# Laying out the solved blocks of a delta-rule recurrence: TensorE products with the unit matrix in place of transfers through DRAM

## The chip, the cores and the metric

One Trainium2 chip, one core of it, float32 throughout. The metric is the device time of one launch in microseconds (us). The kernel before has a median of 3638.72 us over three runs (3634.84 to 3644.53). The kernel computes two whole blocks of a network; the change touches one stage of the first block that takes some 400 us of the time.

## The reference, cut to what matters

The first block mixes tokens by a recurrence (RWKV-7), run forward and backward over 256 context and then 512 latent tokens, 8 heads of 64 in each direction:

```python
def wkv_bidir(r, k_d, v, kk, w, a, state0):
    xs = (tm(both(r)), tm(per(w)), tm(per(k_d)), tm(both(v)), tm(both(-kk)), tm(per(kk[:, :, None] * a)))

    def step(s, inp):
        r_t, w_t, k_t, v_t, aa_t, bb_t = inp
        sa = jnp.einsum('dbhij,dbhj->dbhi', s, aa_t)
        s = s * w_t[..., None, :] + sa[..., :, None] * bb_t[..., None, :] + v_t[..., :, None] * k_t[..., None, :]
        y_t = jnp.einsum('dbhij,dbhj->dbhi', s, r_t)
        return s, y_t

    state, ys = lax.scan(step, state0, xs)
...
    y_c, state_c = wkv_bidir(r_c, k_c, v_c, kk_c, w_c, a_c, state0)
    y_l, _ = wkv_bidir(r_l, k_l, v_l, kk_l, w_l, a_l, state_c)
```

What follows it (group norm, a Fourier mix, a mixture of experts, a second block with sparse attention) is not touched.

## The kernel before, in words

The recurrence is computed in chunks of 64 tokens. A *unit* is 128 tokens (two chunks) in both directions; units 0 and 1 are the context, 2 to 5 the latent tokens. Inside a chunk the tokens depend on each other through a lower triangular matrix per head, which has to be inverted. The kernel does it for all 32 pairs of head and chunk of a unit at once, in parts with names:

- **a1** (`load`, `lora`, `expo1`, `expo2`, `keys1`): the loads of k, kn and r, the decay and rate products, their running sum and its two exponentials.
- **a2** (`keys2` to `keys4`, `gram`, `move`, `turn`): scaled keys on DVE (L651 to L667); the Gram products on PE (L683) and their 24 (context: 16) masks on DVE (L684 to L688); `move` brings the diagonal blocks of 32x32 into the tile `N` through DRAM (`scN`, L695, L698); `turn` transposes the keys (L706).
- **s** (`solve`): 31 steps of two DVE instructions each (L722, L724) that invert the 64 diagonal blocks of the unit, 32 rows of them in `Fm`.
- **b** (`back`): brings the inverted blocks from `Fm` into the layouts that the next products read. Two DVE copies (L733) and nine transfers through DRAM: `scF` (L737), `scE` (L738), `fe` (L739, L740) and the diagonal of `fd` (L745).
- **m** (`merge`, `merge2`): per unit 32 products of 32x32 from `lm` and `fe` (L754), copied to `re` (L755), then 32 more (L764), copied into `fd` (L765): the off-diagonal blocks.
- the **chain** (`fill`, `X`, `V`, `St`, `Y`, L790 to L867): the state's own way through the unit, which needs `v` (loaded at L787), `fd`, `ar`, `bkt`; `St` (L848) makes the next state, `Y` (L866, L867) the output of latent units.

`head()` plays unit 0's a1, a2 and s beside the last projection products. `wkv()` then plays b and m of unit 0 and a2 of unit 1, and after that one *step* for each unit u, in which stand chain(u), s, b and m of unit u+1, a2 of u+2 and a1 of u+3. Each piece has a position between u and u+1 from the table `PL`, and `play` writes the pieces in the order of positions: s of u+1 from 0.127 to 0.312, b at 0.838, the Gram parts of u+2 from 0.885 to 0.942, `turn` at 0.932, m at 0.999. A scheduler then settles the order of instructions inside each engine's queue, and each engine runs its queue in that order. Transfers are issued by SP, in its queue's order.

`ttile` hands out work tiles of 4 KB per partition by turns: 8 in one pool, 4 in another (`nt`, L592). A new tile waits until its predecessor in the same place has been read.

Of the kernel before, what the change touches and what calls it, by code (L numbers as in the profile page):

```python
# [8 lines left out]
F = mybir.dt.float32  # L9
R = mybir.dt.float32r  # L10
I32 = mybir.dt.int32
AF = mybir.ActivationFunctionType
# [86 lines left out]
class Blk1:  # L99
# [432 lines left out]
    def open_wkv(self):  # L532

        tc, nc, I = self.tc, self.nc, self.i
        self.yD = [self.dram.tile([512, 512], F, name=f"yD{d}") for d in range(2)]
        self.prD = self.dram.tile([128, 4, 4, 2, 128], F, name="prD")
        self.vtD = [self.dram.tile([512, 512], F, name=f"vtD{d}") for d in range(2)]
        self.gnD = [[self.dram.tile([128, 512], F, name=f"gnD{d}{u}") for u in range(2, 5)] for d in range(2)]
        wc = self.wA = self.ctx.enter_context(tc.tile_pool(name="wA", bufs=1, side="right", reuse_waits="tile"))
        self.wB = None  # L540
        self.fd = [wc.tile([128, 4, 4, 64], F, name="fd0")]
        nc.gpsimd.memset(self.fd[0], 0.0)
        self.sv = {}
        self.ntt = 0
        self.U = [self.unit(u) for u in range(6)]
# [43 lines left out]

        return (self.wB if u % 3 else self.wA).tile(shape, F, name=name, tag=f"{name}{u % 3}", bufs=1)  # L590

    nt = (8, 4)  # L592

    def unit(self, u):

        nc = self.nc
# [35 lines left out]

        def expo2():
            c = S["c"]
            e1, e2 = S["e1"], S["e2"] = self.tt("e1"), self.tt("e2")
            nc.scalar.activation(e1, c, AF.Exp, scale=-KAP)
            nc.scalar.activation(e2, c, AF.Exp, scale=KAP)
            pcc = S["pc"] = self.wA.tile([128, 4, 4], F, name="pcc", tag="pcc", bufs=4)
            nc.gpsimd.tensor_copy(pcc, e1[:, :, :, 63])
# [69 lines left out]
        def solve(a, b):  # L709

            def f():
                N = S["N"]
                if a == 0:
                    room = self.ttile([128, 2, 16, 32], "Fm")
                    S["F"], S["T"] = room[:, 0], room[:, 1]
                    nc.gpsimd.memset(S["F"], 0.0)
                    for j in range(2):
                        nc.gpsimd.memset(S["F"][j * 64:(j + 1) * 64].rearrange("p s t -> p (s t)")[:, j::34], 1.0)
                Fm, tm = S["F"], S["T"]
                for s in range(a, min(b, 31)):  # L720
                    w, m = 31 - s, s // 2 + 1
# [2 lines left out]
                    nc.vector.tensor_tensor(Fm[:, :m, s + 1:], Fm[:, :m, s + 1:], tm[:, :m, :w], op=OP.add)  # L724
            return f

        def back():
            Fm = S["F"]

            re = S["re"] = self.ttile([128, 32, 32], "re")  # L730
            fe = S["fe"] = self.ttile([128, 32, 32], "fe")
            for a in range(2):
                nc.vector.tensor_copy(re[32:64].rearrange("p t (i a) -> p a i t", a=2)[:, a], Fm[a * 64:a * 64 + 32])  # L733
            scf = self.dram.tile([2, 32, 32, 32], F, name="scF", tag="scF", bufs=3)
            sce = self.dram.tile([32, 32, 32], F, name="scE", tag="scE", bufs=3)
            for a in range(2):
                nc.sync.dma_start(scf.rearrange("b c (i a) t -> a (b c) i t", a=2)[a], Fm[a * 64:(a + 1) * 64])  # L737
            nc.sync.dma_start(sce, re[32:64])  # L738
            nc.sync.dma_start(fe[0:32], scf[1].rearrange("c s t -> s c t"))  # L739
            nc.sync.dma_start(fe[64:96], sce.rearrange("c a b -> a c b"))  # L740
            fd = S["fd"] = self.fd[u % 3]
            for b in range(2):
                for h in range(2):
                    q = h * 64 + 32 * b
                    nc.sync.dma_start(fd[q:q + 32, :, :, 32 * b:32 * b + 32].rearrange("p a n t -> p (a n) t"),  # L745
                                      scf[b, h * 16:h * 16 + 16].rearrange("c s t -> s c t"))

        def merge(q):
            def f():
                re, fe, lm = S["re"], S["fe"], S["lm"].rearrange("p h a n t -> p (h a n) t")  # L750
                p = self.psum()
                for j in range(16):
                    c = q * 16 + j
                    nc.tensor.matmul(p[0:32, j * 32:(j + 1) * 32], lm[64:96, c, 32:64], fe[64:96, c, :], start=True, stop=True)  # L754
                nc.scalar.activation(re[0:32, q * 16:(q + 1) * 16], p[0:32].rearrange("p (c t) -> p c t", t=32), AF.Copy)  # L755
            return f

        def merge2(q):
            def f():
                re, fe = S["re"], S["fe"]  # L760
                p = self.psum()
                for j in range(16):
                    c = q * 16 + j
                    nc.tensor.matmul(p[0:32, j * 32:(j + 1) * 32], re[0:32, c, :], fe[0:32, c, :], start=True, stop=True)  # L764
                nc.scalar.activation(S["fd"][q * 64:q * 64 + 32, :, :, 32:64], p[0:32].rearrange("p (a n t) -> p a n t", n=4, t=32), AF.Copy)  # L765
            return f

        a2 = [keys2, keys3] + ([keys4] if lat else []) + [gram(q) for q in range(4)] + [move, turn]
        sv = list(range(32))
        return {"S": S, "a1": [load, lora(0), lora(1), expo1, expo2, keys1], "a2": a2,  # L770
                "s": [solve(a, b) for a, b in zip(sv, sv[1:])], "b": [back], "m": [merge(0), merge(1), merge2(0), merge2(1)]}

    def slab(self, d, k):
        if (d, k) not in self.sv:
# [2361 lines left out]
```

## Time and profile before

| | |
|---|---|
| median of 3 runs | 3638.72 us (3634.84 to 3644.53) |
| profiled execution, its own time | 3639.38 us |
| its span, first to last instruction | 3637.5 us |
| mean granted TensorE clock | 0.931 |
| PE busy over the span | 3310.7 us (91%) |
| DVE, ACT, POOL busy | 66%, 46%, 28% |
| the stage of the change | about 250 to 664 us |

The profile is one execution. The share of PE over the span is an average over many stages. The recurrence is one of the few in which the PE is idle for longer: of its five steps 0 to 4 (305 to 605 us) PE is busy 228 of 300 us. A step is measured here from the first L790 of a unit to the first L790 of the next, where the chain takes over the next unit. "PEclk" is the clock that TensorE was granted, as a share of 2.4 GHz; 0.50 is 1.2 GHz.

### The profile page before, as it was taken

How to read it: one execution, taken by the hardware profiler on the slowest of the kernel's cores; microseconds unless marked ns; L12 is line 12 of the kernel's file. 1: busy time of each engine (PE TensorE's matmuls, PEld its weight loads, DVE VectorE, ACT ScalarE, POOL GpSimd, SP SyncE). 2: the span in 40 equal slices, each digit the busy share in tenths (PEclk: the TensorE clock that was granted, in tenths of full speed). 3: DMA queues.
4: the chain of work that ended last, by engine and by line, in shares of the span. 5: the costliest groups of instructions: out<-in, count | busy, mean ns of one | idle time of the engine just before them, and what ended most of it. 6: DMA issues, size and time to landing. Idle time of an engine off the chain costs nothing. (4 is left out here: it accounts for less than half of the span.)

```text
span 3637.5 us, 49607 instructions
## 1 busy us (share of the span) xinstructions
PE 3310.7 (91%) x16700; PEld 2483.3 (68%) x16700; DVE 2416.8 (66%) x4743; ACT 1662.0 (46%) x2901; POOL 1017.3 (28%) x960
## 2 busy tenths in 40 slices
PE   7877589949999998999999997999999999999999
PEld 4756477646656565666666564788878878887887
DVE  6787775576978677867867776654656455456653
ACT  4634233314656555554655553444444334444442
POOL 4342122432312211201301313332421433324223
PEclk9986676969999999999999998999999999999999
DMA  7853234626889889789889987322321243222112
GB/s 259 268 162 83 63 73 124 227 81 203 297 304 314 288 307 323 259 293 320 299 286 311 308 271 249 113 81 64 88 61 53 92 141 88 76 76 82 41 53 104
DMA packets 420268, 653.41 MB, mean 180 GB/s; under 512 B 83763, under 2 KB 145264, under 8 KB 419494
## 3 DMA queue, kind: packets, MB, share of 16 engines
q1 hardware_dynamic: 414362, 633.24, 53.8%
q0 software_dynamic: 3920, 13.63, 1.2%
q10 hardware_dynamic: 1724, 3.28, 0.3%
q8 instruction: 135, 2.21, 0.3%
q14 instruction: 127, 1.04, 0.1%
HBM read 610.46 MB, written 39.61 MB: 179 GB/s over the span
## 5 line engine op out<-in xcount | busy, mean ns | idle before, releaser
L1336 DVE TENSOR_TENSOR wlo<-wraw,whi 128x1024 fp32r<-128x1024 f32 (+1 forms) x712 | 855.5, 1212 | 389.4 <-ACT whi L1332 378.0
L1332 ACT ACTIVATE whi<-wraw 128x1024 fp32r<-128x1024 f32 x712 | 741.1, 1056 | 542.7 <-PE ps L1725 141.4
L2302 PE MATMUL psg<-whi,xh 128*128 128x512 f32 (+1 forms) x1152 | 471.4, 409 | 0.8 <-ACT xh L2319 0.8
L2304 PE MATMUL psg<-whi,xl 128*128 128x512 f32 (+1 forms) x1152 | 450.5, 391 | 0.0
L2303 PE MATMUL psg<-wlo,xh 128*128 128x512 f32 (+1 forms) x1152 | 449.1, 390 | 0.3 <-DVE wlo L1336 0.3
L1747 POOL TENSOR_TENSOR ln<-ln,sg 64x256 f32<-64x256 f32 (+1 forms) x148 | 194.8, 1318 | 786.0 <-DVE ln L1746 542.8
L1338 POOL TENSOR_TENSOR wlo<-wraw,whi 128x288 fp32r<-128x288 f32 x184 | 241.3, 1313 | 578.9 <-ACT whi L1332 562.6
L1726 PE MATMUL ps<-wlo,x 128*128 128x512 f32 x864 | 349.7, 405 | 8.2 <-DVE wlo L1336 8.2
L1725 PE MATMUL ps<-whi,x 128*128 128x512 f32 x864 | 352.3, 408 | 0.0
L1721 PE MATMUL ps<-wraw,x 128*128 128x512 f32 x640 | 303.0, 616 | 0.0
L2304 PEld LDWEIGHTS psg<-whi,xl 128*128 128x128 f32 x1152 | 217.1, 188 | 42.1
L2303 PEld LDWEIGHTS psg<-wlo,xh 128*128 128x128 f32 x1152 | 217.7, 189 | 35.2 <-DVE wlo L1336 0.8
L2302 PEld LDWEIGHTS psg<-whi,xh 128*128 128x128 f32 x1152 | 217.6, 189 | 35.4 <-ACT xh L2319 1.8
L1721 PEld LDWEIGHTS ps<-wraw,x 128*128 128x128 f32 x640 | 121.9, 196 | 123.3 <-issue 117.8
L1726 PEld LDWEIGHTS ps<-wlo,x 128*128 128x128 f32 x864 | 166.2, 192 | 52.7 <-DVE wlo L1336 15.7
L1725 PEld LDWEIGHTS ps<-whi,x 128*128 128x128 f32 x864 | 166.7, 193 | 45.0 <-issue 4.8
L1725 PE MATMUL ps<-whi,a 128*128 128x512 f32 x432 | 182.1, 422 | 0.0
L1726 PE MATMUL ps<-wlo,a 128*128 128x512 f32 x432 | 178.1, 412 | 1.5 <-DVE wlo L1336 1.5
L2442 ACT ACTIVATE pexp<-pss,mx 128x128 f32<-128x128 f32 x192 | 100.9, 526 | 155.0 <-DVE mx L2437 66.6
L1721 PE MATMUL ps<-wraw,a 128*128 128x512 f32 x320 | 148.2, 604 | 0.0
L1745 ACT ACTIVATE sg<-gl 64x256 f32<-64x256 f32 (+1 forms) x148 | 61.0, 412 | 147.3 <-DVE gl L1743 140.1
L1693 POOL DMA_INDIRECT xg<-hD,idxi x37 | 46.4, 1255 | 265.6 <-PE ps L1706 239.7
(732 smaller groups left out, 6760.5 us busy)
## 6 DMA issues: line engine op xcount, KB each, us to landing
wraw<-in_w SPq DMA_DIRECT2D x768, 512.0 KB
wraw<-in_w_in SPq DMA_DIRECT2D x140, 512.0 KB
mraw<-in_w_ada SPq DMA_DIRECT2D x32, 512.0 KB
wraw<-in_w_out SPq DMA_DIRECT2D x24, 512.0 KB
wada<-in_w_ada SPq DMA_DIRECT2D x16, 512.0 KB
wraw<-in_w_mem_kv SPq DMA_DIRECT2D x16, 512.0 KB
wraw<-in_w_branch_m SPq DMA_DIRECT2D x8, 512.0 KB
wraw<-in_w_branch_b SPq DMA_DIRECT2D x8, 512.0 KB
```

Source lines behind the costliest of these rows:

```text
L1332: nc.scalar.activation(hi, raw, AF.Copy)
L1336: nc.vector.tensor_tensor(lw[:, :m], rw[:, :m], hw[:, :m].bitcast(F), op=OP.subtract)
L1338: nc.gpsimd.tensor_tensor(lw[:, m:], rw[:, m:], hw[:, m:].bitcast(F), op=OP.subtract)
L1721: nc.tensor.matmul(ps, a, w[:, k], start=s, stop=e)
L1725: nc.tensor.matmul(ps, a, hi[:, k], start=s, stop=False)
L1726: nc.tensor.matmul(ps, a, lo[:, k], start=False, stop=e and not two)
L1745: nc.scalar.activation(sg[:m], gl[:m], AF.Sigmoid, scale=1.702)
L1747: nc.gpsimd.tensor_tensor(ln[:m], ln[:m], sg[:m], op=OP.mult)
L2302: nc.tensor.matmul(p, xh[:, kk], hi[:, k, :n], start=kk == 0, stop=False)
L2303: nc.tensor.matmul(p, xh[:, kk], lo[:, k, :n], start=False, stop=False)
L2304: nc.tensor.matmul(p, xl[:, kk], hi[:, k, :n], start=False, stop=kk == kch - 1)
L2442: nc.scalar.activation(p[:, :n], s[:, :n], AF.Exp, bias=nm, scale=-1.0, accum_out=H["d"][:, i:i + 1])
```

## The change

The transfers of `back` and its two DVE copies go. In their place PE multiplies the solved blocks with the unit matrix, in two groups of products, and ACT copies the products out of PSUM:

- `back0`: 16 products and two copies give `f0`, what `merge` reads (`fe[64:96]` before).
- `back`: 32 pairs of products that accumulate, each pair 64 columns wide, and 20 copies give the diagonal of `fd` and `f1`, what `merge2` reads (`fe[0:32]` before).

All solves work in one tile `fp` with a fixed place, and its work copy `ft` is fixed, too. `fe` and `Fm` are no longer handed out by turns, `re` lies in the first 32 partitions of the unit's own `N`, and the two exponentials are written over their inputs `sw` and `cum`. A latent unit's step takes 10 tiles by turns from 10 (6 and 4) where it took 14 from 12. The position of b in `PL` stays.

```diff
@@ -540,6 +540,10 @@
         self.wB = None
         self.fd = [wc.tile([128, 4, 4, 64], F, name="fd0")]
         nc.gpsimd.memset(self.fd[0], 0.0)
+
+        self.fp = wc.tile([128, 33, 32], F, name="fp")
+        nc.gpsimd.memset(self.fp, 0.0)
+        self.ft = wc.tile([128, 16, 32], F, name="ftm")
         self.sv = {}
         self.ntt = 0
         self.U = [self.unit(u) for u in range(6)]
@@ -589,7 +593,7 @@
 
         return (self.wB if u % 3 else self.wA).tile(shape, F, name=name, tag=f"{name}{u % 3}", bufs=1)
 
-    nt = (8, 4)
+    nt = (6, 4)
 
     def unit(self, u):
 
@@ -632,7 +636,7 @@
 
         def expo2():
             c = S["c"]
-            e1, e2 = S["e1"], S["e2"] = self.tt("e1"), self.tt("e2")
+            e1, e2 = S["e1"], S["e2"] = S["sw"], c
             nc.scalar.activation(e1, c, AF.Exp, scale=-KAP)
             nc.scalar.activation(e2, c, AF.Exp, scale=KAP)
             pcc = S["pc"] = self.wA.tile([128, 4, 4], F, name="pcc", tag="pcc", bufs=4)
@@ -711,11 +715,10 @@
             def f():
                 N = S["N"]
                 if a == 0:
-                    room = self.ttile([128, 2, 16, 32], "Fm")
-                    S["F"], S["T"] = room[:, 0], room[:, 1]
+                    S["F"], S["T"] = self.fp[:, 1:33:2], self.ft
                     nc.gpsimd.memset(S["F"], 0.0)
                     for j in range(2):
-                        nc.gpsimd.memset(S["F"][j * 64:(j + 1) * 64].rearrange("p s t -> p (s t)")[:, j::34], 1.0)
+                        nc.gpsimd.memset(self.fp[j * 64:(j + 1) * 64].rearrange("p s t -> p (s t)")[:, 32 + j:32 + j + 15 * 66 + 1:66], 1.0)
                 Fm, tm = S["F"], S["T"]
                 for s in range(a, min(b, 31)):
                     w, m = 31 - s, s // 2 + 1
@@ -724,51 +727,62 @@
                     nc.vector.tensor_tensor(Fm[:, :m, s + 1:], Fm[:, :m, s + 1:], tm[:, :m, :w], op=OP.add)
             return f
 
-        def back():
-            Fm = S["F"]
-
-            re = S["re"] = self.ttile([128, 32, 32], "re")
-            fe = S["fe"] = self.ttile([128, 32, 32], "fe")
-            for a in range(2):
-                nc.vector.tensor_copy(re[32:64].rearrange("p t (i a) -> p a i t", a=2)[:, a], Fm[a * 64:a * 64 + 32])
-            scf = self.dram.tile([2, 32, 32, 32], F, name="scF", tag="scF", bufs=3)
-            sce = self.dram.tile([32, 32, 32], F, name="scE", tag="scE", bufs=3)
-            for a in range(2):
-                nc.sync.dma_start(scf.rearrange("b c (i a) t -> a (b c) i t", a=2)[a], Fm[a * 64:(a + 1) * 64])
-            nc.sync.dma_start(sce, re[32:64])
-            nc.sync.dma_start(fe[0:32], scf[1].rearrange("c s t -> s c t"))
-            nc.sync.dma_start(fe[64:96], sce.rearrange("c a b -> a c b"))
-            fd = S["fd"] = self.fd[u % 3]
-            for b in range(2):
-                for h in range(2):
-                    q = h * 64 + 32 * b
-                    nc.sync.dma_start(fd[q:q + 32, :, :, 32 * b:32 * b + 32].rearrange("p a n t -> p (a n) t"),
-                                      scf[b, h * 16:h * 16 + 16].rearrange("c s t -> s c t"))
+        def back(g):
+
+            def f():
+                if g == 0:
+                    S["fd"], S["f1"] = self.fd[u % 3], S["f01"][0:32].rearrange("p (t c) -> p t c", c=32)
+                p = self.psum()
+                for j in range(8):
+                    t = 8 * g + j
+                    for a in range(2):
+                        nc.tensor.matmul(p[0:32, j * 64:j * 64 + 64], self.fp[:, 1 - a:33 - a, t], self.ident[:, a * 64:a * 64 + 64], start=a == 0, stop=a == 1)
+                pv = p[0:32].rearrange("p (t b h c) -> p b h c t", b=2, h=2, c=16)
+                for b in range(2):
+                    for h in range(2):
+                        q = h * 64 + 32 * b
+                        nc.scalar.activation(S["fd"][q:q + 32].rearrange("p a n t -> p (a n) t")[:, :, 32 * b + 8 * g:32 * b + 8 * g + 8], pv[:, b, h], AF.Copy)
+                nc.scalar.activation(S["f1"][:, 8 * g:8 * g + 8, :], p[0:32].rearrange("p (t b c) -> p t b c", b=2, c=32)[:, :, 1], AF.Copy)
+            return f
+
+        def back0(g):
+
+            def f():
+                if g == 0:
+                    S["f01"] = self.ttile([128, 1024], "f01")
+                    S["f0"] = S["f01"].rearrange("p (i a c) -> p i a c", a=2, c=32)
+                    S["re"] = S["N"][0:32]
+                p = self.psum()
+                sel = self.ident.rearrange("p (a b c) -> p a b c", a=2, b=2)[:, :, 0]
+                for j in range(8):
+                    nc.tensor.matmul(p[0:32, j * 64:j * 64 + 64].rearrange("p (a c) -> p a c", a=2), S["F"][:, 8 * g + j, :], sel, start=True, stop=True)
+                nc.scalar.activation(S["f0"][64:96, 8 * g:8 * g + 8].rearrange("p i a c -> p (i a c)"), p[0:32], AF.Copy)
+            return f
 
         def merge(q):
             def f():
-                re, fe, lm = S["re"], S["fe"], S["lm"].rearrange("p h a n t -> p (h a n) t")
+                re, f0, lm = S["re"], S["f0"], S["lm"].rearrange("p h a n t -> p (h a n) t")
                 p = self.psum()
                 for j in range(16):
                     c = q * 16 + j
-                    nc.tensor.matmul(p[0:32, j * 32:(j + 1) * 32], lm[64:96, c, 32:64], fe[64:96, c, :], start=True, stop=True)
-                nc.scalar.activation(re[0:32, q * 16:(q + 1) * 16], p[0:32].rearrange("p (c t) -> p c t", t=32), AF.Copy)
+                    nc.tensor.matmul(p[0:32, j * 32:(j + 1) * 32], lm[64:96, c, 32:64], f0[64:96, :, :, c].rearrange("p i a -> p (i a)"), start=True, stop=True)
+                nc.scalar.activation(re[:, q * 16:(q + 1) * 16], p[0:32].rearrange("p (c t) -> p c t", t=32), AF.Copy)
             return f
 
         def merge2(q):
             def f():
-                re, fe = S["re"], S["fe"]
+                re, f1 = S["re"], S["f1"]
                 p = self.psum()
                 for j in range(16):
                     c = q * 16 + j
-                    nc.tensor.matmul(p[0:32, j * 32:(j + 1) * 32], re[0:32, c, :], fe[0:32, c, :], start=True, stop=True)
+                    nc.tensor.matmul(p[0:32, j * 32:(j + 1) * 32], re[:, c, :], f1[:, :, c], start=True, stop=True)
                 nc.scalar.activation(S["fd"][q * 64:q * 64 + 32, :, :, 32:64], p[0:32].rearrange("p (a n t) -> p a n t", n=4, t=32), AF.Copy)
             return f
 
         a2 = [keys2, keys3] + ([keys4] if lat else []) + [gram(q) for q in range(4)] + [move, turn]
         sv = list(range(32))
         return {"S": S, "a1": [load, lora(0), lora(1), expo1, expo2, keys1], "a2": a2,
-                "s": [solve(a, b) for a, b in zip(sv, sv[1:])], "b": [back], "m": [merge(0), merge(1), merge2(0), merge2(1)]}
+                "s": [solve(a, b) for a, b in zip(sv, sv[1:])], "b": [back0(0), back0(1)] + [back(g) for g in range(4)], "m": [merge(0), merge(1), merge2(0), merge2(1)]}
 
     def slab(self, d, k):
         if (d, k) not in self.sv:
```

Line numbers of the changed kernel are 4 higher than before up to `back`, and 14 higher behind it.

The queue of PE in step 0, from the `St` products of the second chunk (L848 before, L862 after) on; ps is PSUM. Before:

```order
L848 MATMUL ps<-uv,bkt 64x64 [waits DVE_49]
L848 MATMUL ps<-uv,bkt 64x64 x3
L683 MATMUL ps<-ar,bk 128x128 [waits PE_49,Pool_49]
L683 MATMUL ps<-ar,bk 128x128 x3
L683 MATMUL ps<-ar,bk 128x128 [waits Pool_49]
L683 MATMUL ps<-ar,bk 128x128 x7
L683 MATMUL ps<-ar,bk 128x128 [waits PE_49]
```

The changed kernel at the same place:

```order
L862 MATMUL ps<-uv,bkt 64x64 [waits DVE_49]
L862 MATMUL ps<-uv,bkt 64x64 x3
L758 MATMUL ps<-ident,fp 32x64 [waits DVE_49,PE_49,Pool_49]
L758 MATMUL ps<-ident,fp 32x64 x7
L758 MATMUL ps<-ident,fp 32x64 [waits PE_49]
L758 MATMUL ps<-ident,fp 32x64 x7
L739 MATMUL ps<-ident,fp 32x64 [waits Activation_49]
L739 MATMUL ps<-ident,fp 32x64 x15
L739 MATMUL ps<-ident,fp 32x64 [waits Activation_49]
...
L862 MATMUL ps<-uv,bkt 64x64 [waits Activation_49]
L862 MATMUL ps<-uv,bkt 64x64 x7
L687 MATMUL ps<-ar,bk 128x128 [waits PE_49,Pool_49]
```

The 80 products stand ahead of the last `St` of the step and of the Gram products of unit u+2 (L687), and the first of them (L758) waits for DVE, which writes `fp`. Before, nothing ahead of the merges (L754, behind the Gram products and `turn`) waited for the solve.

The queue of DVE in step 1, at the solve of unit 2 (L722, L724 before). Before:

```order
L722 TENSOR_TENSOR Fm<-Fm,N 128x9x15
L686 TENSOR_TENSOR ar<-ps,msk 64x512
L724 TENSOR_TENSOR Fm<-Fm 128x9x15
L688 TENSOR_TENSOR lm<-ps,msk 64x256
L722 TENSOR_TENSOR Fm<-Fm,N 128x9x14
L684 TENSOR_TENSOR lm<-ps,msk 64x256
L724 TENSOR_TENSOR Fm<-Fm 128x9x14
```

The changed kernel, at the end of the same solve (L725, L727):

```order
L725 TENSOR_TENSOR ftm<-fp,N 128x16
L664 TENSOR_TENSOR ar<-kn,sw 64x4x4x63
L727 TENSOR_TENSOR fp<-fp,ftm 128x16
L671 TENSOR_TENSOR ar<-r,sw 64x4x4x64 x2
L864 TENSOR_TENSOR pst_3570<-ps,pcc 128x256
L867 TENSOR_TENSOR sv<-pst_3570,pst 64x4x64 x2
L688 TENSOR_TENSOR lm<-ps,msk 64x256
```

Before, the masks of unit 3 (L684 to L688) stood between the instructions of the solve of unit 2; now all of them stand behind it, and behind one `St`.

The queue of SP in step 0 and 1: the loads of `N` (unit 2) and of `v` (unit 1). Before:

```order
L787 DMA v<-vD 128x1024 [waits DMAHW1_49,PE_49]
L669 DMA prD<-kd 128x1024 [waits DMAHW2_49,Activation_49,Pool_49]
L787 DMA v<-vD 128x1024 [waits DVE_49,Activation_49]
...
L695 DMA scN<-lm 32x32x32 [waits DVE_49]
L695 DMA scN<-lm 32x32x32
L604 DMA k<-kD 128x1024 [waits DMAHW7_49,DVE_49,Pool_49]
L604 DMA kn<-knD 128x1024 [waits DMAHW0_49,DVE_49,Pool_49]
L698 DMA N<-scN 64x1024 [waits DMAHW5_49,DMAHW6_49,DMAHW1_49,Activation_49]
L698 DMA N<-scN 64x1024 [waits DMAHW2_49]
```

The changed kernel (prD is the store of L673):

```order
L699 DMA scN<-lm 32x32x32 [waits DVE_49]
L699 DMA scN<-lm 32x32x32 [waits DMAHW3_49]
L673 DMA prD<-kd 128x1024 [waits DMAHW4_49,Activation_49,Pool_49]
L702 DMA N<-scN 64x1024 [waits DMAHW5_49,DMAHW3_49,DMAHW6_49,DMAHW2_49,PE_49]
L702 DMA N<-scN 64x1024
L801 DMA v<-vD 128x1024 [waits DMAHW7_49,DMAHW0_49]
```

`v` of unit 1 stood ahead of unit 2's `scN` and `N`; now it stands behind them and behind prD, and the load of `N` waits for PE, which it did not.

## Rows read from the trace of the kernel before

**Rows 1.** The page, part 1: busy us, share, instructions.
```profile
PE 3310.7 (91%) x16700; PEld 2483.3 (68%) x16700; DVE 2416.8 (66%) x4743; ACT 1662.0 (46%) x2901; POOL 1017.3 (28%) x960
```

**Rows 2.** Windows, by step: us, PE, PEld, DVE, ACT, POOL, PEclk, DMA, GB/s.
```profile
249.90:305.18 55.28, 25.23 (x240) 24.21 (x241) 37.04 (x67) 23.61 (x51) 21.12 (x19) 0.53 0.40 106
305.18:347.29 42.11, 35.09 (x416) 30.82 (x416) 38.84 (x109) 22.10 (x51) 11.73 (x16) 0.74 0.21 39
347.29:431.63 84.34, 35.86 (x418) 31.58 (x416) 71.68 (x170) 22.70 (x52) 18.54 (x18) 0.64 0.31 79
431.63:487.59 55.96, 53.15 (x547) 44.83 (x545) 35.48 (x72) 24.84 (x56) 17.43 (x17) 0.74 0.29 60
487.59:552.08 64.49, 51.09 (x514) 43.16 (x513) 42.49 (x120) 15.26 (x32) 10.69 (x29) 0.69 0.40 99
552.08:605.47 53.39, 52.70 (x454) 38.37 (x452) 24.73 (x77) 17.01 (x40) 6.53 (x9) 0.66 0.44 121
```

**Rows 3.** Waits, 230:660: who, for what: us, times, longest.
```profile
PE ps L754 <- DMA fe<-scE: 64.1, 3, 34.6
```

**Rows 4.** Timeline of PE: start, length, instruction, [idle before, releaser].
```profile
267.12 3.62 PE L754 MATMUL ps<-fe,lm 32*32 32x32 f32 x64 [17.24 <-DMA fe<-scE]
...
305.18 1.89 PE L790 MATMUL ps<-ident,v 128*64 128x128 f32 x8 [12.83 <-DVE Fm L724]
...
340.52 3.46 PE L754 MATMUL ps<-fe,lm 32*32 32x32 f32 x61
...
347.29 1.06 PE L790 MATMUL ps<-ident,v 128*64 128x128 f32 x4
...
424.89 3.43 PE L754 MATMUL ps<-fe,lm 32*32 32x32 f32 x61 [34.57 <-DMA fe<-scE]
...
545.33 3.43 PE L754 MATMUL ps<-fe,lm 32*32 32x32 f32 x61 [12.30 <-DMA fe<-scE]
```

**Rows 5.** Timeline of SP (transfer issues) behind unit 2's solve.
```profile
416.62 1.26 SPq L737 DMA_DIRECT2D scF<-Fm  x2
...
421.51 0.30 SPq L740 DMA_DIRECT2D fe<-scE  x1
```

**Rows 6.** Timeline of DVE: solves of units 1 and 2, last gram mask of unit 2.
```profile
304.13 0.19 DVE L722 TENSOR_TENSOR Fm<-Fm,N 128x31 f32<-128x31 f32 x1 [3.90 <-DMA N<-scN]
...
331.99 0.20 DVE L724 TENSOR_TENSOR Fm<-Fm 128x16 f32<-128x16 f32 x1
...
346.03 0.42 DVE L688 TENSOR_TENSOR lm<-ps,msk 64x256 f32<-64x256 f32 x1
...
368.16 0.19 DVE L722 TENSOR_TENSOR Fm<-Fm,N 128x31 f32<-128x31 f32 x1
...
416.41 0.19 DVE L724 TENSOR_TENSOR Fm<-Fm 128x16 f32<-128x16 f32 x1
```

**Rows 7.** Timeline of PE: small products in fp32 at either clock.
```profile
325.47 1.15 PE L848 MATMUL ps<-uv,bkt 128*64 128x64 f32 x32
...
356.11 3.46 PE L832 MATMUL ps<-xb,fd 128*64 128x128 f32 x15 [4.49 <-DVE xb L818]
...
448.04 0.47 PE L867 MATMUL ps<-uv,lm 64*64 64x64 f32 x2
...
492.27 1.85 PE L832 MATMUL ps<-xb,fd 128*64 128x128 f32 x15 [0.44 <-DVE xb L818]
```

**Rows 8.** Groups by line on ACT, 230:664: busy us, mean ns, idle.
```profile
L622 ACT ACTIVATE sw<-ps,halfb 128x128 f32<-128x128 f32 x40 | 10.9, 381 | 5.9 <-PE ps L619 5.9
...
L755 ACT ACTIVATE re<-ps 32x512 f32<-32x512 f32 x12 | 7.0, 587 | 66.3 <-PE ps L754 66.3
```

**Rows 9.** Timeline of SP: the loads of N (unit 1) and v (unit 0).
```profile
296.44 1.12 SPq L698 DMA_DIRECT2D N<-scN  x2
297.65 0.54 SPq L787 DMA_DIRECT2D v<-vD  x1
```

**Rows 10.** Timeline of POOL ahead of them.
```profile
299.06 3.37 POOL L668 TENSOR_TENSOR kd<-kd,r 128x1024 f32<-128x1024 f32 x1 [4.67 <-DVE bk L652]
```

## The prediction

> **What bounds the kernel now.** I read the page's busy times first: PE is busy 91% of the span [rows 1], so in most of the kernel only PE's work counts. Then the windows by step [rows 2]. In steps 0 to 4 (305.18 to 605.47, 300.3 us) PE is busy 35.1, 35.9, 53.2, 51.1 and 52.7 us, 227.9 in all; 72.4 us are idle, of which 84.34 - 35.86 = 48.5 lie in step 1 and 13.4 in step 3. In the head (249.90 to 305.18) PE has 30 us idle at a mean clock of 0.53. The list of waits names what the change removes: PE waits 64.1 us in three places for `fe` coming through `scE` [rows 3]. The reader is to check in the timeline [rows 4] that these are units 0, 2 and 4 (17.24, 34.57, 12.30); unit 1's merges at 340.52 follow without a wait.
>
> A wait named after a transfer is not all transfer. For unit 2 the last solve instruction on DVE starts at 416.41 [rows 6], `scF` is issued at 416.62, `fe` at 421.51 [rows 5], PE starts at 424.89 [rows 4]: the chain of transfers is 424.89 - 416.6 = 8.3 us; the other 26 of the 34.57 are the solve itself. It takes 368.16 to 416.6, 48.4 us, because DVE's queue has the masks of unit 3 between its instructions. Unit 1's takes 304.13 to 332.19, 28 us, with only the chain's instructions between [rows 6]. So three of the 8 us are what the transfers themselves cost, some 24 us, unless the solve comes earlier or its order changes.
>
> **The change part by part.**
>
> *Removed.* Nine transfers and two DVE copies a unit. The chain of 8.3 us goes where it was waited for: units 0, 2, 4. In the merges of units 1, 3 and 5 nothing was waited for, so there is nothing to win.
>
> *The 80 products of a unit.* Each has a stationary of 128x32 and 64 moving columns, all into partitions 0 to 31. The nearest row is L832: 128 rows, 64 wide, 128 columns, two records a product. 15 records take 1.85 us at 2.4 GHz and 3.46 us at 1.2 GHz [rows 7], so 0.25 and 0.46 us a product; half the columns, 0.123 and 0.231; 80 of them 9.9 or 18.5 us. From below: L848, 64 columns, 16 products in 1.15 us [rows 7], 0.072 each, 5.8 us; but it writes by turns to two halves of the output, which the new ones do not. From above: L867 with L866 at the low clock; two records of L867 start 448.04 and its pair takes up to 0.47 us [rows 7], 38 us. Which clock? After the waits the merges ran at 1.2 GHz (64 records in 3.62 us [rows 4]); L832 behind 4.49 us of idle ran at 1.2 GHz, behind 0.44 us at 2.4 [rows 7]. The products stand behind a wait for the solve, so I take 15 us, nearer to the low clock. The stationary is read with a stride of 32 elements; no row shows that, I take nothing for it, the upper bound covers it.
>
> *The 22 copies of a unit* on ACT: 2 of 32x512 by 587 ns, and 20 smaller ones by at most the 381 ns of a 128x128 [rows 8]: 8.8 us. PE's own 15 us hide them, group by group; ACT has 42 - 22 = 20 us free in step 0 [rows 2]. At 9.9 us for the products they would still fit.
>
> *The order on PE.* This is the term that decides. The products are queued ahead of the last `St` and of the Gram products of unit u+2; their first waits for DVE. So within a step these come one after another: solve of u+1, products, Gram and masks of u+2, `turn`, merges, next step. In step 0 of before, solve's end to the step's end is 332.2 to 347.29 [rows 4, 6], 15.1 us; but the Gram products began at 325.47 + 1.15 = 326.6, before the solve ended (they follow that L848 [rows 7]), so the tail from the first Gram product is 347.3 - 326.6 = 20.7 us. The Trainium skill ("TensorE: Matmul & The Clock Gate", "The mechanism" under packing small matmuls) says that matmuls start and end strictly in queue order. By it a Gram product could not pass a waiting L758; the trace agrees as far as it shows this, since in the 34.57 us of waiting at L754 PE runs nothing else [rows 4]. If a Gram product could pass, the tail would be 15.1 in place of 20.7 us, and the sum 4 x 5.6 = 22 us smaller.
>
> *The order on SP.* `N` of u+2 waits for PE. A latent step takes 10 tiles from 10, so `N` comes to the place of the `N` before it, which the merges now read as `re`: it is issued at the step's end. `v` stands behind it. From issue to use took 304.13 - 296.44 = 7.7 us for `N` and 305.18 - 297.65 = 7.5 us for `v` [rows 4, 6, 9]. So at the start of steps 1 to 3 PE waits some 7 us for `v` and DVE as long for `N`; before, `v` was there. Bounds: 0 and 7.7. In step 0 prD goes ahead of both, and it waits for L668 on POOL, which ends at 299.06 + 3.37 = 302.43 [rows 10]. With 0.3 us for its own issue `N` goes out at 302.7 for 296.44: 6 us later, and `v` with it. That comes on top of the products, since L668 waits for DVE's keys, and these stand behind the masks of the Gram products that the products push back.
>
> *The rest.* Two tiles fewer by turns delay only the loads of k, kn and r for a1, whose uses stand at 0.706 of the next step; I take 0, and if that cover is gone it is one transfer of 7.5 us in a step. 54 transfers fewer on SP, by 0.3 to 0.63 us each to issue [rows 5], free the queue, but it is the waiting in it that counts. One `fp` for all makes the next solve wait for the products' reads; the Gram parts lie between, 0.
>
> *The steps.* Length = landing of `N` 7 (0 to 7.7) + solve 28 + products 15 (9.9 to 18.5) + tail 20.7, or PE's busy time with the products and its wait for `v`, if that is longer.
> - Head: products 15 for some 8 us of transfers (+7), prD (+6): +13 (+2 to +17).
> - Step 0 begins as `v` lands, 1 us behind `N` (304.13 and 305.18): 28 + 15 + 20.7 - 1 = 62.7 for 42.1: +21 (+15 to +24).
> - Step 1: 70.7 for 84.3: -14 (-26 to -9).
> - Step 2: 70.7, or by PE's work 53.2 + 15 + 7 = 75; I take 73 for 56.0: +17 (+7 to +23).
> - Step 3: 70.7, or 51.1 + 15 + 7 = 73; 72 for 64.5: +7.5 (-3 to +13).
> - Step 4 has no Gram behind the products: PE's work 52.7 + 15 = 67.7 for 53.4: +14 (+9 to +18).
> - Step 5 and what follows shift with it.
>
> Sum +58.5 us (+4 to +86). The profiled execution took 3639.4 us, 2 us more than its span and 0.7 us above the median of the runs: 3639.4 + 58.5 = 3698 us, and from the median 3697.
>
> **The rivals.**
>
> *PE-bound, faster (0.10).* The solves run ahead of PE, as unit 3's must have in step 2, the products find `fp` ready at 2.4 GHz, and the waits are gone. Each step is then PE's busy time plus 9.9: 227.9 + 5 x 9.9 - 300.3 = -23, head +2: 3618 us. It decides if `N` lands early in the step. For it: step 2 with 2.8 us idle [rows 2]. Against it: `N` of u+2 is issued only behind the merges of u+1, so a solve cannot start before its own step does.
>
> *Only products and solve (0.13).* `N` and `v` do not wait (another place in the pool, or the merges are early): steps of 62.7, 63.7, 68.2, 66.1 and 67.7 us, that is +21 -21 +12 +2 +14 = +28, and +7 in the head: about 3674 us. For it: no row shows such a wait of `N`. Against it: it is in the queue of SP, with `v` behind it.
>
> *The small products cost more (0.06).* The Trainium skill ("TensorEngine Tiling (Array Packing)", Key Properties) says that a change of tiling mode drains TensorE. In the trace L866 (128*64) and L867 (64*64), which change by turns, need up to 0.47 us a product at the low clock [rows 7], twice what L832's rate gives for the same columns, so it agrees. The 80 products are of one kind, so I hold to L832's rate. If each costs as one of the pairs, 38 instead of 15 us, six units add 138 and the time is about 3836 us.
>
> *No difference (0.06).* What the removed waits give (64.1) pays for the products (6 x 9.9 at the high clock, 59 us): 3635 us. Against it: of the 64.1 only 24 are transfers, and the rest, the solve, is waited for at L758 instead.
>
> The forecast itself has 0.65, with 3657 to 3723 as its own range. Over all, 8 in 10 lie from 3625 to 3730. This kernel's runs differ by some 0.3%, 11 us; faster by more 0.10, within it 0.06, slower 0.84 (the forecast 0.65, the second rival 0.13, the third 0.06).
>
> **What the changed profile would show.** L758 waits for DVE 5 us or more in most steps, and the merges (L768) wait for nothing. The products: 80 in 10 to 18 us a unit. First `fill` (L804) of units 1 to 3: a wait for `v` of about 7 us behind the merges. Steps of 63, 71, 73, 72, 68 us. Wrong, if the solve ends before PE reaches L758 (then the first rival), if `N` is issued well before the merges end (the second), or if the products take 30 us (the third).

## The result, and the profile after

The changed kernel has a median of 3688.1 us (3677.2 to 3696.0, 4 runs) beside 3637.4 us for the kernel before (3634.8 to 3644.5). The ratio is 1.0124, 95% interval 1.0106 to 1.0143: slower by 45 us, 39 to 52. The span of its profiled execution is 3691.0 us, 53.5 more than before.

Nearly all of it lies in the stage of the change. The windows by step of the changed kernel, columns as in [rows 2] (the head from 250.00 on; a step from the first L804 of a unit to the first of the next):

```profile
250.00:314.43 64.43, 36.28 (x402) 35.13 (x402) 37.82 (x70) 30.37 (x73) 21.04 (x19) 0.60 0.21 60
314.43:381.75 67.32, 46.56 (x576) 42.43 (x577) 46.80 (x113) 29.75 (x74) 16.94 (x17) 0.73 0.16 50
381.75:450.54 68.79, 44.70 (x576) 40.81 (x577) 49.01 (x123) 29.56 (x74) 16.94 (x17) 0.75 0.18 57
450.54:521.96 71.42, 63.97 (x705) 55.21 (x705) 46.91 (x110) 31.42 (x78) 16.72 (x18) 0.76 0.20 52
521.96:594.97 73.01, 62.56 (x673) 54.63 (x674) 36.99 (x108) 21.73 (x54) 9.23 (x28) 0.73 0.23 59
594.97:657.28 62.31, 61.25 (x613) 48.18 (x613) 25.02 (x80) 23.85 (x62) 6.47 (x9) 0.72 0.32 93
```

Unit 5 begins at 657.28, before at 605.47: 51.8 of the 53.5 us are lost by then. The steps:

| | before | forecast | after |
|---|---|---|---|
| head ends at | 305.2 | 318 | 314.4 |
| step 0 | 42.1 | 62.7 | 67.3 |
| step 1 | 84.3 | 70.7 | 68.8 |
| step 2 | 56.0 | 73 | 71.4 |
| step 3 | 64.5 | 72 | 73.0 |
| step 4 | 53.4 | 67.7 | 62.3 |

The steps have become alike. Their idle time on PE has not: 72.4 us before, in steps 0 to 4, and 342.8 - 279.0 = 63.8 after, while PE's work in them rose from 227.9 to 279.0. The waits of the changed kernel from 230 to 720 us, columns as in [rows 3]:

```profile
PE ps L804 <- DMA v<-vD: 45.7, 4, 18.6
...
PE ps L758 <- DVE fp L727: 28.3, 4, 9.5
```

The 64.1 us for `fe` [rows 3] are gone; 45.7 us for `v` and 28.3 us for the solve stand in their place. The timeline of PE shows where (columns as in [rows 4]; unit 0's products, step 1 from its start on, unit 3's products in step 2, and the start of step 3):

```profile
259.57 3.37 PE L758 MATMUL ps<-ident,fp 128*32 128x64 f32 x32 [9.52 <-DVE fp L727]
262.77 7.50 PE L739 MATMUL ps<-ident,fp 128*32 128x64 f32 x128
...
381.75 1.89 PE L804 MATMUL ps<-ident,v 128*64 128x128 f32 x8 [10.20 <-DMA v<-vD]
...
411.05 3.59 PE L758 MATMUL ps<-ident,fp 128*32 128x64 f32 x32 [7.96 <-DVE fp L727]
414.44 8.34 PE L739 MATMUL ps<-ident,fp 128*32 128x64 f32 x128
422.70 0.69 PE L862 MATMUL ps<-uv,bkt 128*64 128x64 f32 x16
423.32 5.03 PE L687 MATMUL ps<-ar,bk 64*128 64x128 f32 x64
...
435.47 3.64 PE L778 MATMUL ps<-f,N 32*32 32x32 f32 x61
...
450.54 1.88 PE L804 MATMUL ps<-ident,v 128*64 128x128 f32 x8 [11.43 <-DMA v<-vD]
...
478.86 1.97 PE L758 MATMUL ps<-ident,fp 128*32 128x64 f32 x32
480.67 7.50 PE L739 MATMUL ps<-ident,fp 128*32 128x64 f32 x128
...
521.96 1.46 PE L804 MATMUL ps<-ident,v 128*64 128x128 f32 x6 [5.45 <-DMA v<-vD]
```

The reader is to see the order that the forecast named: wait for the solve (7.96), products (411.05 to 422.7), the last `St` (L862), Gram (L687), merges (they start at 431.88; L778 is their second half), wait for `v` (11.43), next step. In step 2 the wait for the solve is missing: L758 follows the instruction before it at once. The two windows on the products, columns as in [rows 2], give the clock:

```profile
411.00:414.40 3.40, 3.35 (x32) 3.38 (x33) 3.39 (x2) 0.58 (x1) 3.40 (x2) 0.50 0.03 5
414.50:422.60 8.10, 8.10 (x130) 8.10 (x128) 0.83 (x1) 4.89 (x16) 3.05 (x1) 0.90 0.01 2
```

The first 16 products ran at 1.2 GHz, 3.4 us for 16; the other 64 mostly at 2.4 GHz, 8.3 us. Together 11.7 us here and 10.6 in unit 0. In units 3 and 5, whose products stood behind no wait, all 80 ran at 2.4 GHz and took 9.3 and 9.4 us.

### The profile page after: what moved, and what is told of

It is laid out like the page before. It is cut to its first block, busy times and chain, and to the rows that moved or that the text cites. A ratio compares the mean times of both kernels' runs of the same rounds, so it can differ in the third digit from the quotient of the medians.

```text
span 3691.0 us, 51580 instructions
## 1 busy us (share of the span) xinstructions
PE 3369.1 (91%) x17660; PEld 2545.2 (69%) x17660; DVE 2408.8 (65%) x4731; ACT 1702.4 (46%) x3033; POOL 1016.3 (28%) x961
```

## The experiments

Each ran beside the kernel before on the same chip. A gain or loss in us is the ratio's, times 3637; their 95% intervals reach 4 to 8 us to either side, in x2 14, so that a difference of a few us between two runs is not clear of noise by itself. "The changed kernel" stands at +45.

**prD from another queue (x1).**

```diff
-            nc.sync.dma_start(self.prD[:, u - 2]
+            nc.gpsimd.dma_start(self.prD[:, u - 2]
```

> The changed kernel with one edit: the store prD is issued from POOL's queue, so SP no longer has it ahead of N and v. Theory A (a step is a chain of solve, products, Gram, merges, and the loads of N and v are held on SP by prD, which waits for the product on POOL): N of unit 1 is issued at about 298 instead of 307 us, N of unit 4 at about 509 instead of 515, the others 1 us earlier; 10 to 15 us less than the changed kernel, about 3674. Theory B (what is lost is PE's work for 480 products, PE being the bound): no change, within 3 us. Theory C (N waits for the merges, whose tile it takes the place of, as the prediction put it): step 0 gains up to 8 us, steps 1 to 3 nothing.

Ratio 1.0099 (1.0078 to 1.0121), +36: 9 us less than the changed kernel, the median 12 less (3675.8). The two intervals overlap; the traces bear the gain out, for unit 5 begins at 639.78, in the changed kernel at 657.28. The issue of transfers by SP in the changed kernel, in the head and in step 2, columns as in [rows 5]:

```profile
292.68 0.94 SPq L699 DMA_DIRECT2D scN<-lm  x2
306.64 0.34 SPq L673 DMA_DIRECT2D prD<-kd  x1
307.08 1.20 SPq L702 DMA_DIRECT2D N<-scN  x2
308.38 0.55 SPq L801 DMA_DIRECT2D v<-vD  x1
...
503.41 0.94 SPq L699 DMA_DIRECT2D scN<-lm  x2
...
514.92 0.34 SPq L673 DMA_DIRECT2D prD<-kd  x1
515.43 1.12 SPq L702 DMA_DIRECT2D N<-scN  x2
```

and with prD moved, on SP and then on PE at the start of step 0:

```profile
293.51 0.94 SPq L699 DMA_DIRECT2D scN<-lm  x2
296.89 1.09 SPq L702 DMA_DIRECT2D N<-scN  x2
...
497.12 1.11 SPq L702 DMA_DIRECT2D N<-scN  x2
```

```profile
304.38 1.89 PE L804 MATMUL ps<-ident,v 128*64 128x128 f32 x8 [8.00 <-DMA v<-vD]
```

`N` goes out 3.4 us after `scN` (296.89 for 293.51) where it took 14.4, and step 0 begins 10 us earlier. At the ends of steps 0 and 1 prD held `N` by less: 6.4 us from `scN` to `N` in the changed kernel, 4.0 and 3.4 here. The product that prD stores ends on POOL at 512.54 + 2.36 = 514.90 in step 2 of the changed kernel; prD (514.92) and `N` follow at once, `v` at 516.59:

```profile
512.54 2.36 POOL L672 TENSOR_TENSOR kd<-kd,r 128x1024 f32<-128x1024 f32 x1
```

With prD moved the same `N` goes out at 497.12, while the merges of unit 3 run on PE from 495.78 to 503.03: it did not wait for them. Theory C is out, A stands at the lower end of its size. In steps 0 and 1 this run does not tell the two apart, since there `N` goes out 0.8 to 1.3 us behind the merges; x3 does.

**v from POOL's queue, too (x2).**

```diff
-                    nc.sync.dma_start(L["v"].rearrange("p h n t -> p (h n t)"), self.vD[:, u]...
+                    nc.gpsimd.dma_start(L["v"].rearrange("p h n t -> p (h n t)"), self.vD[:, u]...
```

(and prD as in x1.)

> The changed kernel with two edits: prD and the load of v are issued from POOL's queue. Theory A: PE's wait for v at the start of a step (45.7 us in four places) goes almost wholly, but the solve still begins only when N has landed, so that most of it comes back as a wait for the solve at L758; 10 to 20 us less than the changed kernel. A variant of it, in which v and not N sets the step's length: 35 to 45 us less. Theory B: no change.

Ratio 1.0221 (1.0183 to 1.0258), +80: 44 us worse than with prD alone moved. All theories missed. `v` now stands behind prD and its product on POOL, and lands later than `N`. DVE in step 1 of this run:

```profile
386.95 0.24 DVE L725 TENSOR_TENSOR ftm<-fp,N 128x78 f32<-128x78 f32 x1
396.34 0.43 DVE L832 TENSOR_SCALAR xb<-ps 64x256 f32<-64x256 f32 x1 [9.15 <-ACT xb L831]
```

The solve stops for 9.15 us in its middle, since the chain's L832 is queued between its instructions and needs `v`. So a late `v` holds the solve as well, not PE alone.

**v in time, on SP (z3).** The load of `v` of unit u+1 as a piece of its own at half of step u; prD as in x1.

```diff
+        def loadv():
+            S["v"] = self.tt("v")
+            nc.sync.dma_start(S["v"].rearrange("p h n t -> p (h n t)"), self.vD[:, u]...
...
-                put(u, spread(self.chain(self.U[u]["S"]), 0, 1), ...
+                put(u, spread(self.chain(self.U[u]["S"]), 0, 1), spread(get(u + 1, "v"), 0.5, 0.5), ...
```

> The changed kernel with prD from POOL's queue and the load of v of the next unit written at half of a step, on SP. In the run with v and prD on POOL's queue v came later than N, and DVE's solve stood still until the chain's L832 had what it needs, since L832 is queued between the solve's instructions. If that is so, v in time gains: PE's 23 us of waiting for v in the run with prD moved go, and the time is 5 to 20 us below its 3676. If N alone sets the step: within 4 us of 3676. If the slower POOL queue itself was the cause: within 4 us too.

Ratio 1.0133 (1.0110 to 1.0156), +48: 12 us worse than x1, a miss. No wait of PE for `v` is left among its large ones, but this is:

```profile
PE ps L762 <- DVE fp L731: 83.9, 6, 22.1
```

29.7 us in x1, 83.9 here. PE starts its chain earlier and then waits the longer for the solve. The trace shows what else the edit moved. In x1 the solve starts between 2.4 us ahead of and 1.1 us behind the start of its step, here 10.5 to 17.0 us behind it. In step 1, which starts at 368.55, it is

```profile
382.84 0.19 DVE L729 TENSOR_TENSOR ftm<-fp,N 128x31 f32<-128x31 f32 x1
```

because instructions of the chain (L835 to L870), some of which wait for ACT, now stand ahead of it in DVE's queue. `N` of units 4 and 5 goes out 13.3 and 13.4 us after its `scN`, behind transfers of the chain on SP (`vtD`). So the run is no test of `v` alone: it gave up the early solve for the early `v`.

**The products behind the Gram products (x3).**

```diff
-PL = [0.127, 0.312, 0.838,
+PL = [0.127, 0.312, 0.97,
```

> The changed kernel with one number changed: the position of back in the table PL is 0.97 instead of 0.838, so that the 80 products of a unit stand behind the Gram products and turn of the next unit in PE's queue, directly ahead of the merges. The work is the same. Theory A: the Gram products no longer wait for the solve, their masks and the load of N come earlier and the solve can begin earlier; some 8 to 10 us less in each of steps 0 to 3, 25 to 45 us in all, about 3650. Theory B: no change, since PE has the same work.

Ratio 1.0051 (1.0031 to 1.0070), +18.5: 27 us less for one number, at the lower end of A; B is out, the work being the same. PE in step 1 of this run:

```profile
403.52 1.94 PE L710 MATMUL ps<-ident,bk 128*128 128x128 f32 x8 [0.50 <-DVE lm L692]
405.39 2.58 PE L758 MATMUL ps<-ident,fp 128*32 128x64 f32 x32
407.81 7.50 PE L739 MATMUL ps<-ident,fp 128*32 128x64 f32 x128
417.57 3.62 PE L768 MATMUL ps<-f,lm 32*32 32x32 f32 x61 [2.26 <-ACT f L759]
...
425.14 1.25 PE L804 MATMUL ps<-ident,v 128*64 128x128 f32 x5 [0.33 <-DMA v<-vD]
```

`turn` (L710) now stands ahead of the products, these follow without a wait, and the next chain starts 0.33 us after the merges, for 11.43. `N` of unit 3 is issued ahead of the first merge product (417.57), and `N` of unit 2 at 360.11 ahead of the one at 361.62, so they wait for no merge:

```profile
417.38 1.20 SPq L702 DMA_DIRECT2D N<-scN  x2
```

**The wait alone (z2).** The kernel before, transfers and all, with one product that waits where the changed kernel's products stand:

```diff
         def back():
             Fm = S["F"]
+            pw = self.psum()
+            nc.tensor.matmul(pw[0:16, 0:64], Fm[:, :, 31], self.ident[:, 0:64], start=True, stop=True)
```

> The kernel before, with its transfers, and one product more in back: it reads the solved blocks, so PE waits for the solve at the place where the changed kernel has its 80 products, ahead of the Gram products; nothing uses what it makes. Theory A1 (the wait at this place by itself is the loss): 15 to 35 us more than before. Theory A2 (what counts is what PE has to do between the solve's end and the Gram products, 11 us of products, with the order only making them count; the wait alone costs in step 0 and gives back in step 1, where the solve is no longer split by masks): within 10 us of before.

Ratio 1.0013 (1.0000 to 1.0025): +5 us, 0 to 9. Theory A2. The windows by step, columns as in [rows 2]:

```profile
305.36:350.89 45.53, 33.05 (x418) 29.38 (x419) 43.20 (x111) 22.13 (x51) 12.58 (x16) 0.76 0.18 36
350.89:425.72 74.83, 32.40 (x420) 28.85 (x419) 55.55 (x131) 22.86 (x53) 17.56 (x18) 0.66 0.37 95
425.72:478.51 52.79, 50.16 (x546) 41.96 (x547) 45.10 (x108) 24.06 (x55) 17.59 (x15) 0.82 0.32 67
478.51:550.68 72.17, 57.93 (x516) 49.06 (x515) 41.16 (x115) 15.85 (x33) 10.80 (x33) 0.62 0.32 77
550.68:604.89 54.21, 52.91 (x454) 39.41 (x455) 26.09 (x82) 16.44 (x39) 6.55 (x9) 0.66 0.46 125
```

Their sum is 299.5 us, before 300.3. PE does wait for the solve at the new product, nearly as long in all as it waited for `fe` before (64.1 us [rows 3]):

```profile
PE ps L731 <- DVE Fm L724: 56.5, 4, 29.3
```

The longest of these waits is in step 1 (the timeline of PE there):

```profile
398.48 0.37 PE L731 MATMUL ps<-ident,Fm 128*16 128x64 f32 x2 [29.27 <-DVE Fm L724]
...
399.83 7.53 PE L683 MATMUL ps<-ar,bk 64*128 64x128 f32 x64
...
409.94 2.08 PE L757 MATMUL ps<-fe,lm 32*32 32x32 f32 x61 [0.69 <-PE ps L706]
```

But step 1 is 74.8 us for 84.3 [rows 2], step 2 52.8 for 56.0, while step 0 and step 3 are longer (45.5 and 72.2 for 42.1 and 64.5). In step 1 the solve of unit 2 takes 365.3 to 398.3, 33 us for 48.4 [rows 6]: with the Gram products held back, their masks no longer stand between its instructions. The transfers run beside the Gram products (L683) that follow the wait; the merges (L757) wait for them once, 7.7 us, in unit 0. A wait for the solve at this place is given back; that some eleven microseconds of products there are not is what x3, x4 and y2 show. What this run does not have is prD ahead of `N` and `v`, the fixed `fp`, the fewer tiles and ACT's copies. No run takes these last three apart; y1, below, has them all and is as fast as the kernel before, so together with the products they cost there no more than the removal of the transfers gave.

**Fewer products (x4).** One of each pair of `back` left out.

```diff
-                    for a in range(2):
-                        nc.tensor.matmul(..., self.fp[:, 1 - a:33 - a, t], self.ident[:, a * 64:a * 64 + 64], start=a == 0, stop=a == 1)
+                    nc.tensor.matmul(..., self.fp[:, 0:32, t], self.ident[:, 64:128], start=True, stop=True)
```

> The changed kernel without one product of each pair in back: 48 instead of 80 products a unit (the output is then not the reference's, since half of the layout is left out); waits, copies and order as they were. It prices the products where they stand. If all of them are on the path (A and B alike): 32 x 0.117 to 0.23 us = 3.7 to 7.5 us less a unit, 22 to 45 us in all. If something beside them sets the pace there (ACT's copies, DVE): less than 10 us.

Ratio 1.0083 (1.0064 to 1.0102), +30: 15 us less, 22 by the medians (3666.5), for 192 products. That is 0.08 to 0.11 us each, or 37 to 55 us for all 480 if the rest are worth as much. By the traces PE's time for the products fell by 22 us over the six units (from 62.9 to 40.8), so with 15 to 22 us at the end most of a product's time is on the path.

**The products by turns into four partition groups (y2).**

```diff
+                for j in range(8):
+                    for a in range(2):
+                        for k in range(4):
+                            nc.tensor.matmul(p[32 * k:32 * k + 32, j * 64:j * 64 + 64], self.fp[:, 1 - a:33 - a, 8 * k + j], self.ident[:, a * 64:a * 64 + 64], start=a == 0, stop=a == 1)
```

(`back0` likewise into two groups; the copies read from the four groups.)

> The changed kernel with the same 80 products in another order and place: back's four groups of eight pairs go by turns into four partition groups of one PSUM tile (0, 32, 64, 96), back0's two groups by turns into two. In the kernel before L848, which goes by turns to two halves, took 0.072 us a product where one place only takes 0.107 to 0.123. Theory: products to different column groups overlap, a unit's 80 take 4 to 6 us in place of 10.8, and 5 to 7 us less a unit on the path (as the run with 48 products, which saved 22 us, bears out) make 25 to 40 us less, about 3655. Rival: they do not overlap, or ACT's 22 copies, which now all come behind the last product, take the time back: within 8 us of the changed kernel.

Ratio 1.0065 (1.0048 to 1.0082), +24: 21 us less, somewhat short of 25. In their own time the products do what was expected:

```profile
405.04 1.81 PE L759 MATMUL ps<-ident,fp 128*32 128x64 f32 x30 [8.49 <-DVE fp L727]
...
406.66 2.92 PE L738 MATMUL ps<-ident,fp 128*32 128x64 f32 x126
```

405.04 to 409.6, 4.5 us for 80 products, where 411.05 to 422.7 stood above: 7 us less in this unit, 37 us less over the six, of which somewhat over half reached the end.

**Together.** y1: back at 0.97 and prD moved.

> The changed kernel with the two edits that each gained: back at 0.97 (behind the Gram products) and prD from POOL's queue. Theory A: the one shortened the steps and the other mainly the start of step 0 (which lay at 314.3 us in the run with back at 0.97 and at 304.4 in the run with prD moved), so they add up but for 2 or 3 us: about 10 us less than the run with back at 0.97 alone, 3644. If both had removed the same wait: no less than 3652.

Ratio 1.0004 (0.9994 to 1.0015): 17 us less than x3, as fast as the kernel before. They add up; the few us beyond that are within the intervals.

y3: these two and the products by turns.

> All three: back at 0.97, prD from POOL's queue, products by turns into four partition groups. If the theory holds for each of them: about 3644 less 20 to 30, 3615 to 3625, and so faster than the kernel before (3636). If the products by turns gain nothing: 3644.

Ratio 0.9977 (0.9961 to 0.9993), -8: faster than both kernels, but only 10 us less than y1, where 20 to 30 were expected.

y4: the same with `v` ahead, as in z3.

> As the run before it, and the load of v of unit u+1 is written at half of step u as a piece of its own, still on SP. With back behind the Gram products PE waits for v at a step's start for under 1 us in the run with back at 0.97 alone, so nothing is expected there: within 5 us of the run before it, either way. Rival: SP's queue takes v ahead of N's store and its wait for a place holds N: 5 to 20 us more.

Ratio 1.0003 (0.9989 to 1.0017): 9 us worse than y3: the size of the rival, but not its mechanism, since SP issues `N` 3.5 to 6.7 us after `scN`, in y3 3.4 to 8.0. The loss lies in step 0, 81.8 us for 54.1 in y3. The solve of unit 1 starts there 17 us behind the step's start (300.84), behind instructions of the chain on DVE, and with the masks of unit 2 among its own instructions it takes 48.6 us for 29.7. PE waits for it at the products (DVE, then PE):

```profile
317.79 0.19 DVE L729 TENSOR_TENSOR ftm<-fp,N 128x31 f32<-128x31 f32 x1
...
366.59 1.81 PE L763 MATMUL ps<-ident,fp 128*32 128x64 f32 x30 [21.84 <-DVE fp L731]
```

**The merges by turns (z1), and copies out of their way (z4).** z1 writes the 64 merge products of y3 by turns into four partition groups; z4 also puts the 16 copies of the diagonal of `fd` behind `merge2`.

```diff
-                    nc.tensor.matmul(p[0:32, j * 32:(j + 1) * 32], lm[64:96, c, 32:64], ...
+                        nc.tensor.matmul(p[32 * k:32 * k + 32, j * 32:(j + 1) * 32], lm[64:96, c, 32:64], ...
```

```diff
-"m": [merge(0), merge2(0)]
+"m": [merge(0), merge2(0), diag]
```

> The version with back at 0.97, prD from POOL's queue and the products by turns, and now also the 64 products of merge and merge2 by turns into four partition groups (eight copies of 32x256 in place of four of 32x512). A unit's merges took 7.3 us on PE at 1.2 GHz; by turns, as the products did (80 in 4.6 us for 11), about 2.5. If the merges are on the path, 3 to 5 us less a unit: 18 to 28 us less than 3630, so 3602 to 3612. If ACT's copies between merge and merge2 set the pace (2.4 us of waiting for ACT in each unit before): within 6 us of 3630.

Ratio 0.9963 (0.9950 to 0.9976), -13: 5 us less than y3, within the intervals; the second case. The merges of unit 2:

```profile
398.74 1.13 PE L771 MATMUL ps<-f,lm 32*32 32x32 f32 x64 [2.42 <-ACT f L761]
404.08 2.31 PE L783 MATMUL ps<-f,N 32*32 32x32 f32 x64 [4.21 <-ACT N L773]
```

The first 64 records take 1.13 us at a granted clock of 0.97, where 61 took 3.62 in the changed kernel at 0.69; at 0.50, in the head, they take 1.13 us, too. But PE waits 2.42 us for ACT's copies ahead of them and 4.21 us between the two halves.

> The version with everything by turns, and the 16 copies of the diagonal of fd, which nothing needs before the next chain's V, written as a piece of its own behind merge2. In the version before, PE waited 2.4 us at the first merge product and 4.2 us at merge2 in a unit, because 16 of these copies stood in ACT's queue ahead of f0's two and of merge's four. If ACT's queue set the pace of the merges: 4 to 6 us less in each of units 0 to 5, 15 to 30 us less than the version before, a ratio to the kernel before of 0.988 to 0.992. If the solve or the masks set it: within 5 us, a ratio of 0.995 to 0.998.

Ratio 0.9950 (0.9930 to 0.9969), -18, median 3625.5: 5 us less again and again within the intervals: the lower case, though no version has a lower median. Part of what the merges give turns into a wait for `v`, 9.4 us in z1 and here:

```profile
PE ps L815 <- DMA v<-vD: 22.8, 3, 9.5
```

## Why the prediction was right, and where not

The time came out 9 us below the forecast (3688 for 3697), inside its own range; direction, size and place were right. Part of the size is luck: the products and the tail behind them were taken too long and the waits behind the merges too short, and these errors cancel in part. Of the signs that were named, the steps of like length and the waits for `v` are there; the wait of 5 us or more at L758 is there in the head and in steps 0 and 1 only (3.4 us in step 3, none in steps 2 and 4). Point by point:

- *Removed.* The waits for `fe` are gone. That the transfers themselves were 8 us of each of the three, "some 24 us, unless the solve comes earlier or its order changes", holds with the condition only: in z2, with the changed kernel's order, 7.7 us in unit 0 are left of them.
- *The products* were mis-sized: 15 us a unit were taken, 9.3 to 11.7 measured, 62.9 us in all for the 90 taken; the two shortest lie below the range of 9.9 to 18.5. The start at the low clock was right for four units of six; that the granted clock rises again within the products themselves (0.50, then 0.90 in the windows above) was not seen, nor that units 3 and 5 would stand behind no wait.
- *The order on PE.* "This is the term that decides" was half right. The queue runs as forecast, and moving the products gave 27 us. But the wait by itself costs only 0 to 9 us (z2); what decides is what PE has to do between solve and Gram products.
- *The order on SP* is the step that failed: "`N` comes to the place of the `N` before it, which the merges now read as `re`: it is issued at the step's end". No merge held `N` (x1 at 497.12, x3 at 417.38). It is issued late because its source, `scN`, is itself issued only some 3 us ahead of the end of the merges (368.85 and 436.41 in steps 0 and 1), and because prD, which waits for the product on POOL, stands in between: some 11 us in the head, 2 to 3 at the ends of steps 0 and 1, 6 to 9 in step 2. The forecast had prD only once, ahead of step 0. The wait for `v` was forecast at 7 us and was 10.20 and 11.43 at the starts of steps 1 and 2, 5.45 at step 3's. From its issue to its use `v` took 5.3 to 6.5 us, less than the 7 taken; in [rows 4] the wait that gave 7.5 ends with the solve on DVE and not with `v`, so that number was an upper bound. The total came near for other reasons than the ones given.
- *The tail* was 20.7 us by forecast; in step 1 it is 422.70 to 439.1, 16.4 us. With the wait for `v` it is 27.8 us, where 20.7 + 7 = 27.7 were added up: two errors that cancel.
- *The head*: +9.2 for +13. Products of 10.6 us instead of 15 are enough for the difference; no run takes it apart.
- *Step 0 and step 4*: 67.3 for 62.7, 62.3 for 67.7. Step 4 is shorter mostly by the size of the products (9.4 for 15). In step 0 the errors are larger than their sum. A step ends where the next chain starts, so the wait of 10.20 us for `v` at 381.75 lies in step 0, and the forecast counted it in step 1. Term by term step 0 is 29.5 us to the solve's end (27 forecast), 11.3 with the products (15), 16.3 of tail (20.7) and 10.2 of waiting (0).
- *The rivals.* PE-bound and faster: no, though in steps 2 and 4 the solve did end before PE reached L758, this rival's sign, and y3, with as many products, by turns and later in the queue, is 8 us faster than the kernel before. Only products and solve (3674): x1 without prD's wait is there, 3675.8, and PE still waits in it for `v` (three times, 23.3 us), so the same time is not the same mechanism. Products at the price of L866 and L867: no, 0.12 to 0.15 us each. Its price was read too high as well: the 0.47 us of a pair are records that overlap, and the next pair starts 0.40 us after it (448.04, 448.44). No difference: reached with two edits more (y1).

The Trainium skill ("TensorE: Matmul & The Clock Gate", "The mechanism") has the rule that matmuls keep to queue order. It holds here as far as seen: with the wait of 29.27 us in z2, the Gram products follow only behind it. The Trainium skill ("TensorEngine Tiling (Array Packing)", Key Properties) says that tiles operate independently. The trace agrees: 80 products took 4.5 us over four column groups (y2), 11.7 in one.

## What to carry to other kernels

When transfers are replaced by an engine's work, ask first what stands behind that work in its queue: here transfers could run beside the Gram products (z2), while the products ran ahead of them. A wait in a queue may be given back; here work at the same place was not, for the most part. And read an experiment's queues before its time: moving one load (z3, y4) moved the solve behind the chain on DVE. Look, too, at what a transfer stands behind: one store that waits for a product held two loads whose data had been ready for up to 11 us.

## What the runs showed of the hardware

- Products of 128x32 by 64 columns in fp32 took 0.117 us each into one column group (changed kernel, unit 3: two records a product, 128 records in 7.50 us, granted clock 1.00). By turns into four column groups they took 0.033 us each (y2, unit 5: 126 records in 2.09 us, granted clock 1.00).
- A load of `v` took 5.3 to 6.5 us from SP's issue to its use in the changed kernel, and 5.1 to 10.0 us from POOL's issue in x2, four cases each, with PE waiting for it in all of them.
